# A DeepNorm layer on one core: accumulating transfers of the folded weight chunks begin ahead of a group of seven, and a first down block with one folded chunk more

## The chip, the core and the metric

The kernel runs on one core of one Trainium2 chip. TensorE (PE) multiplies, VectorE (DVE) and ScalarE (ACT) work on tiles in SBUF, GpSimd (POOL) and SyncE (SP) issue transfers. The metric is the device time of one execution in microseconds (us); lower is better. A comparison goes by the median of several runs.

## The reference, cut to what matters

One decoder layer in float32, with 256 tokens, width 2048 and a feed-forward width of 5632:

```python
def swiglu(x, w_gu, w_down):
    g, u = jnp.split(x @ w_gu, 2, axis=-1)
    return (jax.nn.silu(g) * u) @ w_down

h = layer_norm(alpha * h + 0.5 * swiglu(h, w_ffn1_gu, w_ffn1_down), ...)
... # retention and sliding-window attention on h @ w_in, gated and mixed
h = layer_norm(alpha * h + mixed, ...)
h = layer_norm(alpha * h + 0.5 * swiglu(h, w_ffn2_gu, w_ffn2_down), ...)
... # gated input embedding
```

The change touches the two feed-forward networks, `f1` and `f2`.

## The kernel before, in words

**Products.** Every float32 operand is split into a high part (rounded to the matmul's fp32r type) and a low part (what is left). A product is three matmuls into one PSUM sum: low by high, high by high, high by low (`Sum.add`, L431 to L433 in the profile). A weight comes in chunks of 512 KB, 128 x 1024 numbers: SP loads the raw chunk (L119), ScalarE casts the high part and VectorE subtracts it from the raw one (`split`, L105 and L106).

**Units.** The weights are a list, `plan`, of units that are taken in order. Each says how many slots of SBUF its load, its making and its keeping take, and how long TensorE works on it, in products (`time`):
- `Single`: one chunk, time 12.
- `Folded`: one chunk, time 12, whose low part VectorE doesn't make. ScalarE writes the raw chunk times -1 into the low part (L169), and a transfer issued by POOL adds the raw chunk to it, with the type's rounding between (L170). Then ScalarE casts the high part (L171).
- `Seven`: a pair of chunks done by seven products in place of eight, time 21. VectorE makes sums of the raw quarters (L226 to L229), the tiles `u` and `v`; ScalarE casts `h`, `hu`, `hv` and `b`, VectorE subtracts `l`, `lu`, `lv` and `b`.
- `Prepared`: a pair whose sums were put in DRAM earlier.

**Blocks.** The gate-up product runs over 11 blocks `j` of 512 columns of the hidden layer; each has 8 pairs of chunks along the width (one chunk of the pair for gate, one for up). The order of pairs from block 1 of `f1` on is "FFSSFSSP": F is a `Single` and a `Folded`, S a `Seven`, P two `Single`s. A chunk is called `f1_gu_1_1_6`: block 1, up, pair 6. In the profile block numbers are left out of weight names (`lf_gu` is a low part of `f1_gu` or `f2_gu`). The down product has two blocks, with the orders `FIRST_DOWN` and `SECOND_DOWN` over 22 pairs; its chunk `f1_down_1_19` belongs to pair 19. Its sevens are pairs 12 to 19. After the last seven of a block `seven_common` combines the sums (`eve`, `evw`, L550).

**The order.** The program is written in one pass, and each engine does its instructions in the order of writing. `fill`, called after every unit is done with, decides what is written: it makes loaded units while those ready amount to less than 45 products, and loads units while those ready and loaded amount to less than 90, as far as the counted slots go. A real slot of the 46 comes free when its last reader is through; a load waits on SP for that. What is loaded next to what, and what stands ahead of what on ScalarE, VectorE, POOL and SP, so follows from the order of `plan`.

**Other transfers on SP.** After each block the product of gate and up is transposed by a transfer (L189, `mf<-wf`).

Of the kernel before, what the change touches and what calls it, by code (L numbers as in the profile page):

```python
# [9 lines left out]
F32R = mybir.dt.float32r  # L10
# [28 lines left out]
SLOTS = 46  # L39


SEVEN = (0, 1, 2, 3)

AHEAD = {1: (4, 5), 2: (4,), 3: (4, 5), 4: (4,), 5: (4, 5), 6: (4,), 7: (4, 5)}
# [3 lines left out]

SEVEN_DOWN = (6, 7, 8, 9)

FIRST_DOWN = "PPPPPPFFSFSPSFSPSFSSPS"
SECOND_DOWN = "PPPSPSPSFSPSFSSPSPPPPP"
LEAD = 4

# [8 lines left out]
def layer(ctx: ExitStack, tc: tile.TileContext, io):  # L63
# [16 lines left out]
    def slot(shape, dt, name):  # L80
        return slots.tile(shape, dt, tag="slot", name=name)
# [6 lines left out]
    plan = []  # L88

    def chunk_of(key):  # L90


        name, at = key[0], key[1:]
        if name.endswith("_gu"):
            j, gu, c = at
            w = io[name][2 * j : 2 * j + 2, gu, c // 2, :, c % 2 * 2 : c % 2 * 2 + 2, :]
            return w.rearrange("g p k n -> p g (k n)")
        if name[-1] == "2":
            j, c = at
            w = io[name[:-1]][j : j + 2, c // 2, :, c % 2 * 2 : c % 2 * 2 + 2, :]  # L100
            return w.rearrange("g p k n -> p g (k n)")
        return io[name][at]

    def split(dst_hi, dst_lo, src, lo_engine=None):
        act.copy(dst_hi, src)  # L105
        (lo_engine or dve).tensor_tensor(dst_lo, src, dst_hi, ALU.subtract)  # L106

    class Chunk:


        def __init__(self, key, pieces=1, queue=None):
            src = chunk_of(key)
            self.key, self.paired = key, key[0].endswith("_gu") or key[0][-1] == "2"
            self.name = "_".join(map(str, key))
            self.raw = slot(list(src.shape), F32, "r" + self.name)
            n = src.shape[2] // pieces
            self.parts = [slice(j * n, j * n + n) for j in range(pieces)]
            for at in self.parts:
                (queue or sync).dma_start(self.raw[:, :, at], src[:, :, at])  # L119
# [7 lines left out]
        def make(self):  # L127
            self.make_hi()
            split(self.hi, self.lo, self.raw)

        def of(self, v, kk):

            if self.paired:
                return v.rearrange("p g (k n) -> p g k n", k=2)[:, :, kk, :]
            return v[:, kk, :]
# [4 lines left out]
    class Single:  # L140


        loads, makes, keeps, time = 1, 2, 2, 12
# [4 lines left out]
        def load(self, **how):  # L148
            self.chunk = Chunk(self.key, **how)
# [1 line left out]
        def make(self):  # L151
            self.chunk.make()

    class Folded:

        loads, makes, keeps, time = 1, 2, 2, 12

        def __init__(self, key):  # L160
            self.key = key

        def load(self, **how):
            self.chunk = Chunk(self.key, **how)

        def make(self):
            c = self.chunk
            c.make_hi()
            act.mul(c.lo, c.raw, -1.0)  # L169
            pool.dma_start(c.lo, c.raw, accum_op=ALU.add)  # L170
            act.copy(c.hi, c.raw)  # L171

    class Turn:

# [28 lines left out]
    class Seven:  # L203
# [4 lines left out]
        loads, makes, keeps, time = 2, 6, 7, 21  # L208
# [37 lines left out]
    class Prepared:  # L246


        loads, makes, keeps, time = 6, 3, 7, 21
# [63 lines left out]
    loaded, ready = [], []  # L313
    room = {"slots": 0, "used": 0, "ahead": 45, "far": 90, "quiet": False}

    def fill(must=False):

        while True:
            queued = sum(u.time for u in ready)
            left = room["slots"] - room["used"]  # L320
            wanted = must and not ready or not room["quiet"] and queued < room["ahead"]
            if loaded and wanted and loaded[0].makes <= left:
                u = loaded.pop(0)
                u.make()
                room["used"] += u.keeps - u.loads
                ready.append(u)
                continue
            first = loaded[0] if loaded else plan[0] if plan else None
            queued += sum(u.time for u in loaded)
            if plan and queued < room["far"] and plan[0].loads + first.makes <= left:  # L330
                u = plan.pop(0)
                u.load()
                room["used"] += u.loads
                loaded.append(u)
                continue
            return

    def make_next():
        u = loaded.pop(0)
        assert u.makes <= room["slots"] - room["used"]  # L340
        u.make()
        room["used"] += u.keeps - u.loads
        ready.append(u)

    def take(key):
        if not ready:
            fill(True)
        u = ready.pop(0)
        assert u.key == key, (u.key, key)
        return u  # L350
# [23 lines left out]
    def features_chunk(key, n_k, rhs, ps):  # L374
        c, chunks = key[-1], n_k // 4
        u = take(key)
        hi, lo = u.chunk.hi, u.chunk.lo

# [64 lines left out]
    def tokens_out(key, n_k, lhs, ps, n=512, before=None):  # L443

        nk = 1024 // n
        sums = [Sum(ps[t][:, :n], n_k) for t in range(2)]
        for c in range(n_k // nk):
            u = take(key + (c,))
            tokens_chunk(u.chunk, c * nk, lhs, sums, (0, 1), range(nk))
            done(u)  # L450
            run_side()

    def block_units(units, keys):

        for kind, p in units:
            if kind == "P":
                plan.extend(Single(keys(n, p)) for n in range(2))
            elif kind == "F":
                plan.extend(of(keys(n, p)) for n, of in enumerate((Single, Folded)))
            else:  # L460
                plan.append((Seven if kind == "S" else Prepared)(keys(0, p), keys(1, p)))

    def block(name, units, keys, lhs, forms, sums, fold, before=None):
# [5 lines left out]
        for j, (kind, p) in enumerate(units):  # L469
            if before is not None:  # L470
                before(j)
            if kind in "PF":
                for n in range(2):
                    u = take(keys(n, p))
                    tokens_chunk(u.chunk, 2 * p, lhs, [sums[t][n] for t in range(2)], (0, 1))
                    done(u)
                    run_side()
                continue
            u = take(keys(0, p))
            a11, a12 = (half_of(lhs(2 * p + e), 0) for e in range(2))  # L480
            a22 = half_of(lhs(2 * p + 1), 1)
            f5, f6, f7, f3 = forms(p)
            q2, q3, q4 = sums[0][0], sums[0][1], sums[1][0]
            steps = [
                (p1, a11, u.b11), (q2, a12, u.b21), (q3, f3, u.b22), (q5, f5, u.t1),
                (p7, f7, u.t3), (p6, f6, u.t2), (q4, a22, u.t4),
            ]
            if p == sevens[-1]:
                steps = [steps[j] for j in (0, 3, 5, 4, 1, 2, 6)]
            for to, left, right in steps:  # L490
                to.add(left, right)
            done(u)
            run_side()
            if p == sevens[-1]:
                fold(p1.ap, p6.ap, p7.ap, q5.ap)
# [38 lines left out]
    def units_of(order, sevens, ahead=()):  # L534

        sevens, ahead = list(sevens), list(ahead)
        plain = [p for p in range(KD // 2) if p not in sevens + ahead]
        of = {"S": sevens, "D": ahead, "P": plain, "F": plain}
        return [(kind, of[kind].pop(0)) for kind in order]
# [21 lines left out]
    def plan_tokens(key, n_k, nk=2):  # L561
        for c in range(n_k // nk):
            plan.append(Single(key + (c,)))
# [373 lines left out]
    def gu_units(name, j):  # L937
        if j == 0:
            return [("P", p) for p in range(KD // 2)]
        if name == "f2" and j in AHEAD:  # L940
            plain = "P" if j < 4 else "F"
            return units_of(*((f"P{plain}SDSDSP", SEVEN[:3]) if j % 2 else (f"P{plain}SSDSSP", SEVEN)), AHEAD[j])
        order = "FFSSFSSP" if name == "f1" or j > 8 else "PFSSFSSP"
        return units_of(order, SEVEN[: order.count("S")])

# [3 lines left out]
    def down_units(n_held):  # L949
# [4 lines left out]
        first, second = [], []  # L954
        for out, order in ((first, FIRST_DOWN), (second, SECOND_DOWN)):
            n = order.count("S")
# [17 lines left out]
    def ffn(name, i, ht, norm, keep, residual, keepers, away):  # L974
# [33 lines left out]
        for j in range(KF // 4):  # L1008
# [22 lines left out]
            def before(u, j=j, offset=KD // 2 - len(units)):  # L1031
# [7 lines left out]
                if j == 0 and u == 7:  # L1039
                    for g in sorted({p // 2 for p in SEVEN}):  # L1040
                        hi, lo = (slot([P, 8, P], F32R, f"{name}f{w}{g}") for w in "hl")
# [136 lines left out]
    GATE_UNITS = units_of("PPSSPSSP", (0, 1, 2, 3))  # L1178
    RET_UNITS = [units_of(order, SEVEN[: order.count("S")]) for order in ("SPSPSPSP", "PSPSPPPP")]
    gate_keys = lambda b: lambda n, p: ("w_in_f2", 29 + 4 * b + 2 * n, p)  # L1180
# [637 lines left out]
    def warm_up():  # L1818

        ps = bank("warm")  # L1820
        for _ in range(WARM):
            pe.transpose(ps[:, :P], ident, ident)

    with tc.manual_schedule():
# [10 lines left out]
        for blk in range(2, 4):  # L1835
            plan_tokens(("w_pg", blk), KD)
        kept = sorted({p // 2 for p in SEVEN})
        warm_up()
# [105 lines left out]
```

## Time and profile before

| | |
|---|---|
| median of 3 runs | 2230.45 us (2227.97 to 2230.84) |
| the profiled execution | 2230.62 us |
| its span, from the first to the last instruction | 2228.6 us |
| mean granted clock of TensorE | 0.999 |
| TensorE busy | 2218.5 us, 10140 matmuls |
| VectorE busy | 2004.0 us, 90% |
| ScalarE busy | 1439.0 us, 65% |
| GpSimd busy | 50.9 us, 2% |
| moved by DMA | 570.51 MB, mean 256 GB/s |
| accumulating transfers of gate-up chunks | 42 of 512 KB, 8.2 us median from issue to landing |

A stall of TensorE is read where two matmuls that follow each other start further apart than their neighbours. The waits name the instruction that came last before the late one; the chain of waits follows that back to where the delay came from. SPq in a row is SP's queue, where a transfer's issue waits its turn.

### The profile page before, as it was taken

What the parts mean: (1) busy time and instruction counts of PE and PEld (TensorE: products, weight loads), DVE (VectorE), ACT (ScalarE), POOL (GpSimd) and SP (SyncE); (2) the same over time, 40 slices, a digit from 0 to 9 for tenths busy, and PEclk for the clock granted to TensorE, in tenths of its full rate; (3) what the DMA queues carried; (4) which work ended last, traced back from release to release, by engine and by line L of the source; (5) the groups of instructions that cost most, each with busy time, mean ns of one, the idle gap of its engine ahead of it and who ended that gap; (6) DMA issues with size and microseconds to landing.
All of it is one profiled execution on the core that took longest, in us unless ns stands there. A gap on an engine that the chain in (4) does not pass through costs nothing.

```text
span 2228.6 us, 29103 instructions
## 1 busy us (share of the span) xinstructions
PE 2218.5 (100%) x10140; PEld 1838.9 (83%) x10140; DVE 2004.0 (90%) x2624; ACT 1439.0 (65%) x1677; POOL 50.9 (2%) x65
## 2 busy tenths in 40 slices
PE   9999999999999999999999999999999999999998
PEld 8888888888888888888788888888888888888887
DVE  6999999989998789789999888779999999999977
ACT  6777777777565545557865567466766677765653
POOL 0000000000000000000000000000000000000000
PEclk9999999999999999999999999999999999999999
DMA  9988998976686889757976568888999999666871
GB/s 321 250 264 252 249 263 241 269 227 217 228 305 234 298 283 338 203 179 232 291 233 226 184 203 321 316 302 266 301 301 295 300 248 276 209 233 221 309 283 68
DMA packets 302075, 570.51 MB, mean 256 GB/s; under 512 B 98652, under 2 KB 103388, under 8 KB 301928
## 3 DMA queue, kind: packets, MB, share of 16 engines
q1 hardware_dynamic: 291880, 536.71, 72.3%
q0 software_dynamic: 8064, 29.36, 7.0%
q10 hardware_dynamic: 1984, 2.58, 0.4%
q8 instruction: 79, 1.29, 0.2%
q14 instruction: 68, 0.56, 0.1%
HBM read 487.32 MB, written 31.46 MB: 233 GB/s over the span
## 4 chain that ended last, share of the span: by engine, by line
PE 93%; DMA 3%; DVE 2%; issue 1%; ACT 0%; SPq 0%; ACTq 0%; POOL 0%; DVEq 0%; POOLq 0%
PE rqk L382 3%; PE f2g L431 3%; PE f2g L433 3%; PE f2g L432 3%; PE f1g L431 2%; PE f1g L433 2%; PE f1g L432 2%; PE f2u L431 2%; PE f2u L433 2%; PE f2u L432 2%; PE f1u L433 2%; PE f1u L431 2%; PE f1u L432 2%; PE aqk L382 2%; PE f2e L431 1%; PE f1e L431 1%
## 5 line engine op out<-in xcount | busy, mean ns | idle before, releaser
L106 DVE TENSOR_TENSOR lf_gu<-rf_gu,hf_gu 128x1024 fp32r<-128x1024 f32 (+1 forms) x225 | 267.7, 1210 | 22.1 <-ACT hf_gu L105 21.1
L105 ACT CAST hf_gu<-rf_gu 128x1024 fp32r<-128x1024 f32 (+1 forms) x225 | 228.7, 1039 | 22.1 <-DMA rf_gu<-in_f_gu 21.5
L106 DVE TENSOR_TENSOR lw_in_f<-rw_in_f,hw_in_f 128x1024 fp32r<-128x1024 f32 x140 | 167.8, 1219 | 15.0 <-ACT hw_in_f L105 15.0
L106 DVE TENSOR_TENSOR lf_down<-rf_down,hf_down 128x1024 fp32r<-128x1024 f32 x130 | 155.7, 1220 | 12.9 <-ACT hf_down L105 11.1
L105 ACT CAST huf_gu<-uf_gu 128x1024 fp32r<-128x1024 f32 x76 | 80.1, 1053 | 125.4 <-DVE uf_gu L227 109.4
L105 ACT CAST hf_down<-rf_down 128x1024 fp32r<-128x1024 f32 x130 | 132.7, 1049 | 30.5 <-DMA rf_down<-in_f_down 21.3
L105 ACT CAST hw_in_f<-rw_in_f 128x1024 fp32r<-128x1024 f32 x140 | 140.4, 1049 | 2.3 <-PE gt L433 1.6
L105 ACT CAST hvf_gu<-vf_gu 128x1024 fp32r<-128x1024 f32 x76 | 80.1, 1054 | 32.4 <-DVE vf_gu L229 30.5
L106 DVE TENSOR_TENSOR luf_gu<-uf_gu,huf_gu 128x1024 fp32r<-128x1024 f32 x76 | 92.6, 1218 | 0.0
L106 DVE TENSOR_TENSOR lvf_gu<-vf_gu,hvf_gu 128x1024 fp32r<-128x1024 f32 x76 | 92.6, 1218 | 0.0
L431 PE MATMUL f1g<-hf_gu,xt 128*128 128x512 f32 x232 | 90.8, 391 | 0.0
L433 PE MATMUL f1g<-lf_gu,xt 128*128 128x512 f32 x232 | 90.5, 390 | 0.0
L432 PE MATMUL f1g<-hf_gu,xt 128*128 128x512 f32 x232 | 90.5, 390 | 0.0
L431 PE MATMUL f2g<-hf_gu,ht 128*128 128x512 f32 x211 | 82.2, 390 | 0.0
L433 PE MATMUL f2g<-lf_gu,ht 128*128 128x512 f32 x211 | 82.1, 389 | 0.0
L432 PE MATMUL f2g<-hf_gu,ht 128*128 128x512 f32 x211 | 82.1, 389 | 0.0
L433 PE MATMUL f1u<-lf_gu,xt 128*128 128x512 f32 x192 | 75.0, 391 | 1.2 <-DMA lf_gu<-rf_gu 1.2
L431 PE MATMUL f1u<-hf_gu,xt 128*128 128x512 f32 x192 | 74.7, 389 | 0.0
L432 PE MATMUL f1u<-hf_gu,xt 128*128 128x512 f32 x192 | 74.7, 389 | 0.0
L170 POOL DMA_DIRECT2D lf_gu<-rf_gu x42 | 36.4, 867 | 1641.2 <-DMA rf_gu<-in_f_gu 1017.6
L105 ACT CAST huf_down<-uf_down 128x1024 fp32r<-128x1024 f32 x32 | 33.7, 1054 | 60.7 <-DVE uf_down L227 58.7
L1057 ACT ACTIVATE eve<-eve 128x1024 f32<-128x1024 f32 x20 | 21.2, 1061 | 67.3 <-DVE eve L1056 67.3
(1512 smaller groups left out, 6978.3 us busy)
## 6 DMA issues: line engine op xcount, KB each, us to landing
rf_gu<-in_f_gu SPq DMA_DIRECT2D x361, 512.0 KB
rf_down<-in_f_down SPq DMA_DIRECT2D x176, 512.0 KB
rw_in_f<-in_w_in_f SPq DMA_DIRECT2D x148, 512.0 KB
lf_gu<-rf_gu POOLq DMA_DIRECT2D x42, 512.0 KB, 8.2
rw_rv<-in_w_rv SPq DMA_DIRECT2D x32, 512.0 KB
rw_ret<-in_w_ret SPq DMA_DIRECT2D x32, 512.0 KB
rw_mix<-in_w_mix SPq DMA_DIRECT2D x32, 512.0 KB
rw_pg<-in_w_pg SPq DMA_DIRECT2D x32, 512.0 KB
```

The lines of the kernel that those rows point to most:

```text
L105: act.copy(dst_hi, src)
L106: (lo_engine or dve).tensor_tensor(dst_lo, src, dst_hi, ALU.subtract)
L170: pool.dma_start(c.lo, c.raw, accum_op=ALU.add)
L382: pe.matmul(ps[f], hi[:, kk, f * P : (f + 1) * P], rhs(k), start=k == 0, stop=k == n_k - 1,)
L431: pe.matmul(o, al, bh, start=first, stop=False)
L432: pe.matmul(o, ah, bh, start=False, stop=False)
L433: pe.matmul(o, ah, bl, start=False, stop=self.left == 0)
L1057: act.activation(g, g, AF.Silu)
```

## The change

A folded chunk becomes two units. `Folding` loads the raw chunk, has ScalarE write the low part times -1 and POOL issue the accumulating transfer; its time is 0. `Folded` only casts the high part and is taken as before. `fold_at` puts the `Folding` into `plan` ahead of its chunk: 12 products or more ahead, and where there is a `Seven` among the 12 units of `plan` before that place (or at it), ahead of the last such `Seven`. `Folded` stays at the chunk's own place. `fill` passes over units without time. `FIRST_DOWN` gets another order: the first fold comes one pair earlier, there are six F in place of five, and the sevens stand one place earlier or so.

```diff
+FOLD_AHEAD = 12, 12
...
-FIRST_DOWN = "PPPPPPFFSFSPSFSPSFSSPS"
+FIRST_DOWN = "PPPPPFFSFSFSPSFSPSFSPS"
...
-    class Folded:
-        loads, makes, keeps, time = 1, 2, 2, 12
+    class Folding:
+        loads, makes, keeps, time = 1, 1, 2, 0
...
-        def load(self, **how):
-            self.chunk = Chunk(self.key, **how)
+        def load(self):
+            self.chunk = Chunk(self.key)
 
         def make(self):
             c = self.chunk
-            c.make_hi()
+            c.lo = slot(list(c.raw.shape), F32R, "l" + c.name)
             act.mul(c.lo, c.raw, -1.0)
             pool.dma_start(c.lo, c.raw, accum_op=ALU.add)
+
+    class Folded:
+        loads, makes, keeps, time = 0, 1, 2, 12
...
+        def make(self):
+            c = self.chunk = self.begun.chunk
+            c.hi = slot(list(c.raw.shape), F32R, "h" + c.name)
             act.copy(c.hi, c.raw)
+            room["used"] -= self.begun.keeps
+
+    def fold_at(ahead, key):
+        begun = Folding(key)
+        at, time = len(plan), 0
+        while at > 0 and time < ahead:
+            at -= 1
+            time += plan[at].time
+        if ahead and any(isinstance(u, Seven) for u in plan[at - 12 : at + 1]):
+            while not isinstance(plan[at], Seven):
+                at -= 1
+        plan.insert(at, begun)
+        plan.append(Folded(begun))
...
     def make_next():
...
-        ready.append(u)
+        if u.time:
+            ready.append(u)
 
     def take(key):
-        if not ready:
+        while not ready:
             fill(True)
...
             elif kind == "F":
-                plan.extend(of(keys(n, p)) for n, of in enumerate((Single, Folded)))
+                plan.append(Single(keys(0, p)))
+                fold_at(FOLD_AHEAD[keys(1, p)[0][-3:] == "_gu"], keys(1, p))
```

What moves, at three places. First ScalarE in block 1 of `f1`, around the seven of pair 1 and the folded pair 6 behind it. Before:

```order
L105 CAST hf1_gu_1_0_1_576<-rf1_gu_1_0_1_472 128x1024
L105 CAST bf1_gu_1_0_1_580<-rf1_gu_1_1_1_474 128x512
L105 CAST huf1_gu_1_0_1_583<-uf1_gu_1_0_1_570 128x1024
L105 CAST hvf1_gu_1_0_1_587<-vf1_gu_1_0_1_571 128x1024
L105 CAST hf1_gu_1_0_6_607<-rf1_gu_1_0_6_539 128x1024
L169 ACTIVATE lf1_gu_1_1_6_639<-rf1_gu_1_1_6_553 128x1024
L171 CAST hf1_gu_1_1_6_638<-rf1_gu_1_1_6_553 128x1024
```

And with the change:

```order
L170 ACTIVATE lf1_gu_1_1_6_570<-rf1_gu_1_1_6_475 128x1024
L107 CAST hf1_gu_1_0_1_579<-rf1_gu_1_0_1_477 128x1024
L107 CAST bf1_gu_1_0_1_583<-rf1_gu_1_1_1_479 128x512
L107 CAST huf1_gu_1_0_1_586<-uf1_gu_1_0_1_573 128x1024
L107 CAST hvf1_gu_1_0_1_590<-vf1_gu_1_0_1_574 128x1024
L107 CAST hf1_gu_1_0_6_610<-rf1_gu_1_0_6_541 128x1024
L187 CAST hf1_gu_1_1_6_641<-rf1_gu_1_1_6_475 128x1024
```

The negated copy of chunk 1_1_6, with its transfer behind it, has moved from behind the seven's four casts to ahead of them.

Second SP between block 1 and block 2 of `f1`: the loads of the last seven (pair 3), of the last pair (7) and of the next block's folded pairs (4 and 5). Before:

```order
L119 DMA rf1_gu_1_0_3_611<-in_f1_gu 128x2x512
L119 DMA rf1_gu_1_1_3_613<-in_f1_gu 128x2x512
L189 DMA_TRANSPOSE mf10_615<-wf10_555 128x16x128
L119 DMA rf1_gu_1_0_7_643<-in_f1_gu 128x2x512
L119 DMA rf1_gu_1_1_7_687<-in_f1_gu 128x2x512
L119 DMA rf1_gu_2_0_4_722<-in_f1_gu 128x2x512
L119 DMA rf1_gu_2_1_4_743<-in_f1_gu 128x2x512
```

And with the change:

```order
L121 DMA rf1_gu_2_1_4_614<-in_f1_gu 128x2x512
L121 DMA rf1_gu_2_1_5_616<-in_f1_gu 128x2x512
L219 DMA_TRANSPOSE mf10_618<-wf10_555 128x16x128
L121 DMA rf1_gu_1_0_3_643<-in_f1_gu 128x2x512
L121 DMA rf1_gu_1_1_3_645<-in_f1_gu 128x2x512
L121 DMA rf1_gu_1_0_7_647<-in_f1_gu 128x2x512
L121 DMA rf1_gu_1_1_7_691<-in_f1_gu 128x2x512
```

The folded chunks 2_1_4 and 2_1_5 are now loaded ahead of the transposing transfer, and the two chunks of the last seven behind it.

Third SP at the end of the first down block of `f1`. Before:

```order
L119 DMA rf1_down_0_20_4717<-in_f1_down 128x1024
L119 DMA rf1_down_1_20_4777<-in_f1_down 128x1024
L119 DMA rf1_down_0_17_4779<-in_f1_down 128x1024
L119 DMA rf1_down_1_17_4781<-in_f1_down 128x1024
L119 DMA rf1_down_0_18_4803<-in_f1_down 128x1024
L119 DMA rf1_down_1_18_4805<-in_f1_down 128x1024
L119 DMA rf1_down_0_21_4911<-in_f1_down 128x1024
L119 DMA rf1_down_1_21_4938<-in_f1_down 128x1024
L119 DMA rf1_down_0_19_4965<-in_f1_down 128x1024
L119 DMA rf1_down_1_19_4967<-in_f1_down 128x1024
```

And with the change:

```order
L121 DMA rf1_down_1_20_4740<-in_f1_down 128x1024
L121 DMA rf1_down_0_17_4742<-in_f1_down 128x1024
L121 DMA rf1_down_1_17_4744<-in_f1_down 128x1024
L121 DMA rf1_down_0_20_4766<-in_f1_down 128x1024
L121 DMA rf1_down_0_18_4833<-in_f1_down 128x1024
L121 DMA rf1_down_1_18_4835<-in_f1_down 128x1024
L121 DMA rf1_down_0_21_4853<-in_f1_down 128x1024
L121 DMA rf1_down_1_21_4911<-in_f1_down 128x1024
L121 DMA rf1_down_0_19_4913<-in_f1_down 128x1024
L121 DMA rf1_down_1_19_4915<-in_f1_down 128x1024
```

The folded chunk 1_20 is loaded first and 0_20 behind the seven of pair 17, as that seven now stands ahead of pair 20. The last seven's loads (pair 19) keep their place at the end; the slots for them are those of other tiles than before.

More of the change, by code (lines that the diff above doesn't have):

```diff
@@ L152, in make, with __init__, load @@
             self.chunk.make()
-    class Folded:
-        loads, makes, keeps, time = 1, 2, 2, 12
+    class Folding:
+        loads, makes, keeps, time = 1, 1, 2, 0
         def __init__(self, key):
             self.key = key
-        def load(self, **how):
-            self.chunk = Chunk(self.key, **how)
+        def load(self):
+            self.chunk = Chunk(self.key)
         def make(self):
             c = self.chunk
-            c.make_hi()
+            c.lo = slot(list(c.raw.shape), F32R, "l" + c.name)
             act.mul(c.lo, c.raw, -1.0)
             pool.dma_start(c.lo, c.raw, accum_op=ALU.add)
-            act.copy(c.hi, c.raw)
+    class Folded:
+        loads, makes, keeps, time = 0, 1, 2, 12
+        def __init__(self, begun):
+            self.key, self.begun = begun.key, begun
+        def load(self):
+            pass
+        def make(self):
+            c = self.chunk = self.begun.chunk
+            c.hi = slot(list(c.raw.shape), F32R, "h" + c.name)
+            act.copy(c.hi, c.raw)
+            room["used"] -= self.begun.keeps
[10 more added lines that the diff above has]
+        plan.append(Folded(begun))
     class Turn:
@@ L322, in fill @@
             if loaded and wanted and loaded[0].makes <= left:
-                u = loaded.pop(0)
-                u.make()
-                room["used"] += u.keeps - u.loads
-                ready.append(u)
+                make_next()
                 continue
@@ L342, in make_next @@
         room["used"] += u.keeps - u.loads
-        ready.append(u)
+        if u.time:
+            ready.append(u)
     def take(key):
-        if not ready:
+        while not ready:
             fill(True)
```

## The prediction

> **What bounds the kernel now.** I read the page first (busy times), then the waits of TensorE, then the TensorE timeline around each wait, the chain of waits back from there, and last the tables by stretch of time.
>
> Part 1 of the page:
>
> ```profile
> PE 2218.5 (100%) x10140; PEld 1838.9 (83%) x10140; DVE 2004.0 (90%) x2624; ACT 1439.0 (65%) x1677; POOL 50.9 (2%) x65
> ```
>
> PE is busy for 2218.5 of 2228.6 us: 10.1 us of the span are not matmul. Since the change removes no matmul, it can only win time that TensorE loses. The waits of TensorE that the change can reach (released by, us in total, times, longest):
>
> ```profile
> PE f1u L433 <- DMA lf_gu<-rf_gu: 1.2, 2, 0.9
> PE f1e L431 <- DVE evw L550: 0.6, 1, 0.6
> PE f2e L431 <- DVE evw L550: 0.5, 1, 0.5
> ```
>
> The first is a wait for an accumulating transfer (the low part of a folded chunk), the other two are for VectorE at the end of the first down block of either FFN.
>
> Three stretches, each with its length, the busy time (and number) of PE, PEld, DVE, ACT and POOL, then clock, DMA share and GB/s:
>
> ```profile
> 40.00:80.00 40.00, 39.12 (x173) 32.08 (x172) 34.88 (x44) 28.92 (x33) 2.12 (x3) 1.00 1.01 300
> 120.00:160.00 40.00, 40.00 (x178) 33.14 (x177) 37.87 (x46) 29.85 (x34) 2.60 (x3) 1.00 0.91 259
> 540.00:575.00 35.00, 35.00 (x156) 28.81 (x154) 31.29 (x35) 22.09 (x25) 0.86 (x1) 1.00 0.74 243
> ```
>
> The busy time hides part of such a stall, so I measure it from start to start in the TensorE timeline (start us, us, instruction, idle before and its releaser):
>
> ```profile
> 73.21 0.39 PE L431 MATMUL f1u<-hf_gu,xt 128*128 128x512 f32 x1
> 73.43 0.39 PE L432 MATMUL f1u<-hf_gu,xt 128*128 128x512 f32 x1
> 74.70 0.50 PE L433 MATMUL f1u<-lf_gu,xt 128*128 128x512 f32 x1 [0.88 <-DMA lf_gu<-rf_gu]
> 75.04 0.39 PE L431 MATMUL f1u<-hf_gu,xt 128*128 128x512 f32 x1
> ...
> 237.81 0.39 PE L432 MATMUL f1u<-hf_gu,xt 128*128 128x512 f32 x1
> 238.54 0.50 PE L433 MATMUL f1u<-lf_gu,xt 128*128 128x512 f32 x1 [0.34 <-DMA lf_gu<-rf_gu]
> ...
> 401.65 0.39 PE L432 MATMUL f1u<-hf_gu,xt 128*128 128x512 f32 x1
> 401.96 0.50 PE L433 MATMUL f1u<-lf_gu,xt 128*128 128x512 f32 x1
> ...
> 574.81 0.39 PE L433 MATMUL f1e<-lf_down,f1ah 128*128 128x512 f32 x1
> 575.79 0.50 PE L431 MATMUL f1e<-hf_down,f1al 128*128 128x512 f32 x1 [0.59 <-DVE evw L550]
> ...
> 2012.27 0.39 PE L433 MATMUL f2e<-lf_down,f2ah 128*128 128x512 f32 x1
> 2013.18 0.50 PE L431 MATMUL f2e<-hf_down,f2al 128*128 128x512 f32 x1 [0.52 <-DVE evw L550]
> ```
>
> Undisturbed matmuls start 0.22 to 0.23 us apart (73.21 to 73.43; as a mean 40.00 / 178 = 0.225 in the second stretch). The five late ones start 1.27, 0.73, 0.31, 0.98 and 0.91 us after their predecessor, so they are 1.05, 0.50, 0.08, 0.75 and 0.68 us late, together 3.06. The third has no releaser in its row; it is the same matmul of block 9 and I count it with the first two. Each late one lasts 0.50 rather than 0.39 and the next starts 0.34 after it (74.70 to 75.04) rather than 0.225: another 0.11 five times, 0.55. **All five stalls cost 3.6 us, 0.16% of the time.**
>
> **The change part by part.**
>
> *The fold begins earlier.* The chain of waits ahead of the first two stalls (start us, us, what), and the late end of the first down block:
>
> ```profile
> 62.48 0.97 ACT lf_gu L169
> 63.73 10.93 DMA lf_gu<-rf_gu
> ...
> 208.10 9.48 DMA rf_gu<-in_f_gu
> ...
> 229.58 8.92 DMA lf_gu<-rf_gu
> ...
> 557.97 0.03 PE f1d0s L433
> 558.00 5.72 DMA rf_down<-in_f_down
> 563.84 0.69 DVE uf_down L226
> ...
> 573.92 1.22 DVE lf_down L106
> 575.13 0.61 DVE evw L550
> ```
>
> In block 1 the negated copy ran at 62.48 and its transfer took from 63.73 to 74.66; the matmul followed at 74.70. On ScalarE that copy (chunk 1_1_6) stood behind the four casts of the seven before it; now it stands ahead of them. ScalarE runs the four one by one as VectorE makes their sums, so the move is worth the time that a seven takes on TensorE, less what is queued before: 7 products of 3 matmuls of 0.225 us are 4.7 us. The start of the transfer moves from 63.7 to about 59, its end from 74.7 to about 70 at the same length. At 8.92 (block 5) and 10.93 us (block 1), against lateness of 0.50 and 1.05, 4.7 us are ample. So the stalls at 73.43, 237.81 and 401.65 go: 1.63 + 3 × 0.11 = 1.96 us. The landing times of all 42 accumulating transfers of the gate-up blocks:
>
> ```profile
> L169 ACT ACTIVATE lf_gu<-rf_gu x42: 1050/1056/1077, 38.0 to 1870.3; 128x1024 fp32r<-128x1024 f32 x42
> ...
> L170 POOL DMA_DIRECT2D lf_gu<-rf_gu x42: 859/859/1007, 39.4 to 1871.7; - x42
> ...
> DMA to landing us min/median/max: 5.1/8.2/10.9
> ```
>
> At a median of 8.2 and a worst of 10.9, only the third pair of a block ever came too late; the first two pairs had been in time already, so for those the move brings nothing.
>
> *What is moved past.* Each fold issues four things: the load of its raw chunk on SP, the negated copy on ScalarE, the transfer on POOL, and later the cast of the high part. The copy (1.056 us) now stands in ScalarE's queue ahead of the last seven's casts, two of them where both folds of the next block come there, 2.1 us. What hides it (ScalarE and VectorE around the last seven of block 3, and TensorE's use of its last sum):
>
> ```profile
> 153.25 1.05 ACT L105 CAST hf_gu<-rf_gu 128x1024 fp32r<-128x1024 f32 x1
> ...
> 157.51 1.05 ACT L105 CAST huf_gu<-uf_gu 128x1024 fp32r<-128x1024 f32 x1 [2.70 <-DVE uf_gu L227]
> ...
> 156.14 0.68 DVE L226 TENSOR_TENSOR uf_gu<-rf_gu,rf_gu 128x512 f32<-128x512 f32 x1
> ...
> 161.67 1.22 DVE L106 TENSOR_TENSOR lvf_gu<-vf_gu,hvf_gu 128x1024 fp32r<-128x1024 f32 x1
> ...
> 165.28 0.39 PE L433 MATMUL f13s<-lvf_gu,f1fh 128*128 128x512 f32 x1
> ```
>
> ScalarE is idle for 2.70 us before 157.51, in wait for VectorE: two copies at 2.1 us fit in. VectorE's last low part ends at 162.89, 2.39 us ahead of its use at 165.28. So even if the copies pushed all four casts by 2.1 us, nothing would reach TensorE. I put this at nothing; without either cover it would cost at most 2.1 us a block.
>
> On POOL the issue takes 0.86 to 1.01 us, and POOL is 2% busy: nothing. The transfers per FFN grow by one (the first down block folds six chunks, not five). That takes one subtract off VectorE and adds a copy on ScalarE; both lie beside matmuls: nothing.
>
> *On SP* the raws of the next block's folded chunks now go ahead of the last seven's raws, and these come behind the transposing transfer. SP around the place in before:
>
> ```profile
> 132.83 3.84 SPq L119 DMA_DIRECT2D rf_gu<-in_f_gu  x4
> 140.80 2.91 SPq L189 DMA_TRANSPOSE mf<-wf  x1
> 143.81 23.45 SPq L119 DMA_DIRECT2D rf_gu<-in_f_gu  x12
> ```
>
> The last seven's raws were among the four that started at 132.83; now they start behind the transposing at about 143.8, when the following raws start now. At the landing time of 5.72 us that a raw took above they are there at 149.5, at the longest shown, 9.48, at 153.3. ScalarE reads the first at 153.25 and VectorE at 156.14. So the raws arrive in time, but a margin of 11 us has become one of about 4 us.
>
> The DMA engines are full from 40 to 80 us (share 1.01) and nearly so later (0.91). An early fold then doesn't only gain: while it moves its 512 KB, raw loads in the same stretch may land later. I bound this between nothing (the total of bytes is the same but for two transfers) and the 10.93 us of the slowest transfer for a raw, which the margins in the rows above just hold; I take the middle of 5.72 and 9.48, about 7.5 us. A rule speaks here against the change: by the Trainium skill, "DMA: Bandwidth & Descriptors", section "Issuing engines are not separate DMA queues", transfers of all issuing engines run on the same 16 DMA engines and interleave, so that issuing from POOL doesn't keep a fold out of the way of SP's loads. The trace agrees where it shows the share of 1.01 and the 10.93 us in the same 40 us; by this rule alone the gain would be smaller by what the displaced loads cost.
>
> *The first down block.* In the chain above a matmul of the seven of pair 17 ends at 557.97 and frees a slot, the raw of the last seven (pair 19) starts at 558.00, lands at 563.72, and VectorE starts on it at 563.84. VectorE had been idle before that (the row of its timeline):
>
> ```profile
> 563.84 0.69 DVE L226 TENSOR_TENSOR uf_down<-rf_down,rf_down 128x512 f32<-128x512 f32 x1 [3.29 <-DMA rf_down<-in_f_down]
> ```
>
> It had waited 3.29 us for that raw. From there the chain runs through VectorE to `evw`, which ends at 575.74; TensorE starts at 575.79. Now the seven of pair 17 stands ahead of the folded pair 20 on TensorE, and the loads of pair 19 behind fewer others. In matmuls counted between release and use, its two raws gain 18, 4.1 us, against 0.75 late. The DMA engines have room there (share 0.74 in the third stretch). So this stall goes, 0.75 + 0.11, and its twin in the other FFN, 0.68 + 0.11: 1.65 us. What is late next there is `evw` itself, which then waits for TensorE's sums and ScalarE's copy rather than for VectorE's queue. **Sum**: 1.96 + 1.65 = 3.6 us at most; 0.2 off for what remains of a lateness somewhere, 3.4. The profiled execution took 2230.62 us (0.17 above the median of the runs, 2230.45), so **2227.2 us**.
>
> **The rivals.**
>
> *Slower: the last sevens starve.* The mechanism is the displaced raw load: issued behind two folded raws and the transposing transfer, and into DMA engines that an early fold fills. It decides where the landing takes over 153.25 − 143.8 = 9.5 us for ScalarE, or 12.3 us for VectorE plus the 2.39 us left at TensorE: about 14.7 us. Then TensorE waits in the last seven of each gate-up block with folds at its end, some 17 of them. At 0.5 us each this is 8.5 us: 2230.62 − 3.4 + 8.5 = 2235.7. For it: the full DMA share, and the 9.48 us that a raw took before. Against: 14.7 us is beyond every landing shown. Chance 0.15.
>
> *No change: the stall only moves.* The third pairs arrive in time, but VectorE is 34.88 to 37.87 of 40 us busy, and another low part becomes the late one in the same blocks. TensorE then loses again 2 to 3 us: 2229.5 to 2231. For it: VectorE at 37.87 of 40. Against: its queue loses work rather than gains any, and the 2.39 us above. Chance 0.12.
>
> That the change doesn't do what it says I exclude: the order of the instructions shows the copies ahead of the sevens.
>
> **How the numbers follow.** Forecast, stalls gone: 0.68, with a range of its own of 2224.4 (lowest run before, 2227.97, less 3.6) to 2229.5. Slower rival 0.15, no change 0.12, something not seen here 0.05. The three runs of before span 2.87 us; 0.2%, 4.46 us, is about what a measurement of this kernel can tell from no change. Faster by that means below 2225.99, 1.2 us under the forecast: the stalls alone don't reach it, a low run does. Of the forecast's 0.68 I give 0.24 to faster and 0.44 to same; with 0.12 same, 0.15 slower, and the unseen 0.05 split 0.02, 0.01, 0.02: faster 0.26, same 0.57, slower 0.17. The range runs from 2224.4 up into the slower rival, to where 17 blocks lose 0.4 us each (6.8): 2230.62 − 3.4 + 6.8 = 2234.0.
>
> **What would show it.** Right: the waits of TensorE no longer list the transfer of `lf_gu`, nor `evw` at the end of the first down blocks; the copies of the third pairs begin near 58 us rather than 62.48 in block 1; the first load of pair 19 starts near 554. Wrong: new waits of TensorE in the last sevens, with releasers VectorE or ScalarE that had waited for a raw load of over 10 us; a landing time of the accumulating transfers well above the median of 8.2; or the same five stalls at the same length.

## The result, and the profile after

The changed kernel takes 2243.32 us (median of 22 runs, 2228.89 to 2266.1), the kernel before 2228.88 (22 runs, 2226.1 to 2233.15). The ratio is 1.0064, with a 95% interval of 1.005 to 1.0077: slower by 0.6%, where 0.1 to 0.2% faster was forecast. Besides, the runs spread over 37 us in place of 7. The highest, 2266.1, counts as a slow run and isn't in the ratio; the other 21 spread over 31 us. The profiled execution is one of the higher ones: 2253.94 us, with a span of 2252.2.

Busy times (part 1 of the page) and the waits of TensorE, with the change:

```profile
PE 2226.0 (99%) x10140; PEld 1843.7 (82%) x10140; DVE 2000.9 (89%) x2622; ACT 1440.8 (64%) x1679; POOL 52.6 (2%) x67
...
PE f1u L461 <- DMA lf_gu<-rf_gu: 10.5, 2, 7.6
PE f17s L461 <- DVE lf_gu L108: 4.3, 1, 4.3
PE f11s L461 <- DVE lf_gu L108: 2.2, 1, 2.2
```

Both waits for `evw` are gone, as forecast. Of the three for the third accumulating transfer, the two of blocks 5 and 9 are gone; that of block 1 has grown, and block 7 has one of 7.6 us that was none before. Behind each of the two comes a wait in the same block's last seven. TensorE's timeline in block 1 and block 7:

```profile
73.63 0.39 PE L460 MATMUL f1u<-hf_gu,xt 128*128 128x512 f32 x1
76.87 0.50 PE L461 MATMUL f1u<-lf_gu,xt 128*128 128x512 f32 x1 [2.85 <-DMA lf_gu<-rf_gu]
...
85.91 0.39 PE L460 MATMUL f11s<-hf_gu,xt 128*128 128x512 f32 x1
88.52 0.50 PE L461 MATMUL f11s<-lf_gu,xt 128*128 128x512 f32 x1 [2.23 <-DVE lf_gu L108]
...
327.27 0.39 PE L460 MATMUL f1u<-hf_gu,xt 128*128 128x512 f32 x1
335.30 0.79 PE L461 MATMUL f1u<-lf_gu,xt 128*128 128x512 f32 x1 [7.64 <-DMA lf_gu<-rf_gu]
335.89 0.63 PE L459 MATMUL f1u<-hf_gu,xt 128*128 128x512 f32 x1
...
345.17 0.39 PE L460 MATMUL f17s<-hf_gu,xt 128*128 128x512 f32 x1
349.86 0.50 PE L461 MATMUL f17s<-lf_gu,xt 128*128 128x512 f32 x1 [4.29 <-DVE lf_gu L108]
```

What block 7 costs is read from the matmuls done in 40 us, before and after (a stretch, its length, busy time and number for PE, PEld, DVE, ACT, POOL, then clock, DMA share, GB/s):

```profile
320.00:360.00 40.00, 40.00 (x178) 33.10 (x178) 37.73 (x47) 30.60 (x33) 2.62 (x3) 1.00 0.90 255
```

```profile
0.00:320.00 320.00, 312.52 (x1362) 257.06 (x1363) 278.94 (x334) 228.54 (x249) 18.95 (x27) 0.99 0.92 258
320.00:360.00 40.00, 27.29 (x94) 21.05 (x93) 20.55 (x25) 16.35 (x17) 1.77 (x2) 0.79 1.08 201
```

94 matmuls instead of 178: 84 × 0.225 = 18.9 us lost in one block. Up to 320 us 1362 stand against 1394 before, 7.2 us, nearly all of it in block 1 (54 against 84 from 70 to 90 us). Together 26; the span grew by 23.6, and the stalls that went give about the difference back. Part of the loss is the clock: granted 0.79 here on average. After the 7.64 us of idling the matmuls start 0.43 to 0.59 us apart (335.30, 335.89, 336.32) rather than 0.225. By the Trainium skill, "TensorE: Matmul & The Clock Gate", section "Part 1: The HAM clock gate (the "warmup" mystery)", an idle window of about 3.4 us halves TensorE's clock; the trace agrees, with a granted clock of 0.54 and 0.50 from 330 to 340 us in the rows below.

Block 7 by 5 us with the change:

```profile
310.00:315.00 5.00, 5.00 (x23) 4.14 (x23) 4.93 (x7) 5.00 (x6) 0.86 (x1) 1.00 0.74 203
315.00:320.00 5.00, 5.00 (x23) 4.13 (x22) 5.00 (x6) 4.63 (x6) 0.00 (x0) 1.00 1.24 186
320.00:325.00 5.00, 5.00 (x23) 4.13 (x22) 4.86 (x8) 2.63 (x3) 0.00 (x0) 1.00 1.41 45
325.00:330.00 5.00, 2.66 (x12) 1.88 (x10) 2.34 (x3) 1.39 (x2) 1.77 (x2) 1.00 1.18 71
330.00:335.00 5.00, 0.00 (x0) 0.00 (x0) 0.00 (x0) 0.00 (x0) 0.00 (x0) 0.54 1.48 39
335.00:340.00 5.00, 4.70 (x11) 3.73 (x12) 0.00 (x0) 0.00 (x0) 0.00 (x0) 0.50 0.70 158
```

The two last numbers of a row tell it: from 320 to 335 us the times of the packets add up to more than the 16 DMA engines have (1.18 to 1.48), and yet only 39 to 71 GB/s are moved, where 255 were usual in this stretch before. Which transfers had begun by then is in SP's and POOL's rows, first before, then with the change:

```profile
305.82 5.05 SPq L189 DMA_TRANSPOSE mf<-wf  x1
...
311.64 0.86 POOL L170 DMA_DIRECT2D lf_gu<-rf_gu  x1 [17.73 <-ACT lf_gu L169]
```

```profile
313.04 4.87 SPq L219 DMA_TRANSPOSE mf<-wf  x1
318.01 36.81 SPq L121 DMA_DIRECT2D rf_gu<-in_f_gu  x12
...
313.15 0.86 POOL L171 DMA_DIRECT2D lf_gu<-rf_gu  x1 [26.35 <-DVE lvf_gu L108]
...
DMA to landing us min/median/max: 5.4/8.7/22.1
```

Before, the third accumulating transfer of a block began 5.8 us behind the transposing transfer and right behind the end of its issue. Now both start within 0.11 us of each other, and the accumulating one takes 22.1 us, the longest of all (10.9 was the longest before). From 318 to 335 us the transfer queues show (packets by size; then for each queue its packets, MB and share of the 16 engines' time):

```profile
DMA packets 1314, 0.87 MB, mean 51 GB/s; under 512 B 1160, under 2 KB 1160, under 8 KB 1313
...
q1 hardware_dynamic: 1170, 0.34, 96.4%
q0 software_dynamic: 143, 0.52, 35.8%
```

q1 is SP's queue: nearly all its packets are the small ones of the transposing transfer, and of the raw loads behind them hardly a packet moves. Together the queues move 51 GB/s, a fifth of the usual 255. q0 holds the accumulating transfer. The raws of the last seven, issued from 318.01 on, so come some 25 us after their issue (ScalarE's timeline and the chain):

```profile
343.39 1.05 ACT L107 CAST hf_gu<-rf_gu 128x1024 fp32r<-128x1024 f32 x1 [17.00 <-DMA rf_gu<-in_f_gu]
...
319.23 26.49 DMA rf_gu<-in_f_gu
```

My first theory, **A**: where the accumulating and the transposing transfer move data at once, both collapse, and with them the loads queued behind. Its rivals: **B**, the displaced raw loads of the last sevens are the cost in themselves; **C**, the first down block's new order.

### The profile page after: what moved, and what is told of

The parts are those of the page before. It is cut to its first block, busy times and chain, and to the rows that moved or that the text cites. A ratio compares the mean times of both kernels' runs of the same rounds, so it can differ in the third digit from the quotient of the medians.

```text
span 2252.2 us, 29136 instructions
## 1 busy us (share of the span) xinstructions
PE 2226.0 (99%) x10140; PEld 1843.7 (82%) x10140; DVE 2000.9 (89%) x2622; ACT 1440.8 (64%) x1679; POOL 52.6 (2%) x67
## 4 chain that ended last, share of the span: by engine, by line
PE 92%; DVE 3%; DMA 3%; issue 1%; ACT 0%; SPq 0%; ACTq 0%; DVEq 0%
DMA rf_gu<-in_f_gu 3%; PE rqk L410 3%; PE f2g L459 3%; PE f2g L461 3%; PE f2g L460 3%; PE f2u L459 2%; PE f2u L461 2%; PE f2u L460 2%; PE f1g L461 2%; PE f1g L459 2%; PE f1g L460 2%; PE f1u L460 2%; PE f1u L461 2%; PE f1u L459 2%; PE aqk L410 2%; PE f2e L460 1%
## 5 line engine op out<-in xcount | busy, mean ns | idle before, releaser
L108 DVE TENSOR_TENSOR lw_in_f<-rw_in_f,hw_in_f 128x1024 fp32r<-128x1024 f32 x140 | 167.8, 1219 | 14.8 <-ACT hw_in_f L107 14.6
L108 DVE TENSOR_TENSOR lf_down<-rf_down,hf_down 128x1024 fp32r<-128x1024 f32 x128 | 154.0, 1220 | 16.0 <-ACT hf_down L107 14.3
L461 PE MATMUL f1u<-lf_gu,xt 128*128 128x512 f32 x192 | 76.5, 398 | 10.5 <-DMA lf_gu<-rf_gu 10.5
L256 DVE TENSOR_TENSOR uf_gu<-rf_gu,rf_gu 128x512 f32<-128x512 f32 x76 | 52.1, 686 | 36.6 <-DMA rf_gu<-in_f_gu 36.6
```

The source lines that it names most:

```text
L256: dve.tensor_tensor(t1, b11, b12, ALU.add)
L461: pe.matmul(o, ah, bl, start=False, stop=self.left == 0)
```

## The experiments

**Which part of the change.** Only the first down block changed:

```diff
-FOLD_AHEAD = 12, 12
+FOLD_AHEAD = 12, 0
```

> Only the first down block is changed; the accumulating transfers of gate-up chunks begin where they began before. Theory A (the loss is a collision: an accumulating transfer that moves its data at the same time as the transposing transfer slows both, and the raw loads queued behind them): 2226 to 2229 us, no stall of TensorE over 2 us in the gate-up blocks, and the stall at the end of the first down block gone (1.65 us gained). Theory B (the raw loads of the last sevens are displaced on SP): the same, since they stand where they stood. Theory C (the new order of the first down block costs the time): 2240 or more, spread as wide as with the whole change.

Measured 2227.64 us (2225.43 to 2229.28; ratio 0.9995, 0.9987 to 1.0004). Only the gate-up chunks folded ahead:

```diff
-FOLD_AHEAD = 12, 12
+FOLD_AHEAD = 0, 12
-FIRST_DOWN = "PPPPPFFSFSFSPSFSPSFSPS"
+FIRST_DOWN = "PPPPPPFFSFSPSFSPSFSSPS"
```

> Only the gate-up chunks are folded ahead; the first down block is as before. Theories A and B: 2240 to 2248 us with runs spread over 30 us or so, stalls of TensorE of several us in single gate-up blocks. Theory C: 2227 to 2229.

Measured 2243.64 us (2236.52 to 2252.52; 1.0073, 1.0052 to 1.0094): all of the loss. C falls. In its profile, taken in the fastest of the six runs, one accumulating transfer takes 16.4 us.

**Taking one partner away.** The transposing replaced by a plain transfer of the same bytes:

```diff
-            sync.dma_start_transpose(
...
+            sync.dma_start(
...
```

> The changed kernel, with the transposing transfer replaced by a plain transfer of the same 512 KB between the same tiles (so the hidden layer is left untransposed). SP's order and all bytes are the same. Theory A: the long stalls go, 2225 to 2228 us, runs within 6 us of each other, accumulating transfers land within 11 us. Theory B: no change against the whole change, 2240 to 2246, since the raw loads stand where the change put them.

Measured 2225.53 us (2224.96 to 2226.13; 0.9986, 0.9977 to 0.9994). The loads stand on SP where the change put them, so B doesn't explain the loss. The edit reaches all 38 transposing transfers of the program, 22 of them in the feed-forward networks, so the 3.2 us under before needn't all come from there; but no wait of TensorE for an accumulating transfer is left. The spread shrinks to 1.2 us. It is likely, but not shown, that part of the scatter of the kernel before comes from the transposing transfers too: no run takes them out of it. Its accumulating transfers:

```profile
DMA to landing us min/median/max: 4.8/8.3/10.9
```

The accumulating transfer made plain:

```diff
-            pool.dma_start(c.lo, c.raw, accum_op=ALU.add)
+            pool.dma_start(c.lo, c.raw.bitcast(F32R))
```

> The changed kernel, with the accumulating transfers turned into plain ones of the same bytes on the same queue (so the low part of a folded chunk is the raw chunk). Theory A in the narrow form (it is the adding that collides with the transposing): 2225 to 2228 us and no stall over 2 us. Theory A in the wide form (any transfer issued by POOL beside the transposing one): 2238 to 2246. Theory B: 2240 to 2246.

Measured 2226.92 us (2224.66 to 2229.11; 0.9993, 0.9984 to 1.0001). By the time the narrow form of A holds, but not quite by the landings:

```profile
DMA to landing us min/median/max: 2.9/6.3/14.3
```

A plain transfer from POOL can be caught beside the transposing one too (14.3 against a median of 6.3); it is shorter, and caught less badly, and only 0.5 us of wait is left.

**Making the collision in the kernel before.** There only the transposing transfer is moved, one unit of a block later and then two (`later(DELAY, turn.move)`), and with it ScalarE's two copies of its result (`later(DELAY + 3, joined)`):

```diff
-DELAY = 1
+DELAY = 2
```

> The kernel before, with the transposing transfer written one unit of a block later (DELAY 2 for 1), about 4.7 us; nothing is folded earlier. It then starts about 1 us ahead of the third accumulating transfer of a block, as in the changed kernel, where it started 4 to 7 us ahead. Theory A (collision): slower than before, 2235 to 2245 us, with runs spread over 15 us or more, and accumulating transfers of over 15 us. Theory B (displaced raw loads): within 2 us of 2228.7, since the raw loads keep their places but for one that now goes ahead of the transposing.

> The kernel before, with the transposing transfer two units later (DELAY 3). It is now written behind the third negated copy, and both transfers start within 3 us of each other in most blocks; no load of a fold is moved ahead. Theory A (collision): slower than with DELAY 2 (2235.6), 2240 to 2265 us, several accumulating transfers over 14 us. Theory B: within 3 us of 2228.5.

Measured 2235.63 us with DELAY 2 (2230.76 to 2240.55; 1.0028, 1.0019 to 1.0036) and 2253.76 with DELAY 3 (2250.7 to 2256.95; 1.011, 1.0094 to 1.0125). No load of a fold is moved ahead here, so the collision is enough by itself. DELAY 2 brought the two less close than I had expected: the third accumulating transfers start 2.7 to 7.2 us behind the transposing ones, not 1. One block collapses (14.6 us to landing, a wait of 5.8 us), and the runs spread over 9.8 us, not 15. With DELAY 3, in block 10 (SP, POOL, TensorE, waits):

```profile
429.66 6.59 SPq L189 DMA_TRANSPOSE mf<-wf  x1
...
431.91 0.86 POOL L170 DMA_DIRECT2D lf_gu<-rf_gu  x1 [17.62 <-ACT lf_gu L169]
...
453.93 0.80 PE L433 MATMUL f1u<-lf_gu,xt 128*128 128x512 f32 x1 [13.23 <-DMA lf_gu<-rf_gu]
...
PE f1u L433 <- DMA lf_gu<-rf_gu: 13.2, 1, 13.2
PE f2u L433 <- DMA lf_gu<-rf_gu: 9.9, 1, 9.9
```

Two blocks collapse, though the two transfers start within 2.3 us of each other in 13: not every overlap is a collapse.

**Parting them in the changed kernel.** Three ways: the transposing two units later (`DELAY = 3`), the third fold a seven earlier (`FOLD_AHEAD = 12, 36`), the transposing one unit earlier (`DELAY = 0`).

> The changed kernel, with the transposing transfer two units later (DELAY 3), about 9 us, when the third accumulating transfer has landed (7 to 9 us after its issue where nothing collides); the next block's first two then start 3.5 us behind it. Theory A: 2225 to 2229 us, long stalls gone, if 3.5 us behind is far enough; else still some blocks at 15 us and 2232 to 2240. Theory B: the raws of the last sevens stay displaced behind the two folded raws: 2240 or more.

> The changed kernel, with folds of gate-up chunks 36 products ahead in place of 12: only the third of a block moves, ahead of one seven more, so that its accumulating transfer starts about 4.7 us earlier, 3.5 us ahead of the transposing one. Theory A: fewer overlaps, 2226 to 2235. Theory B: no better than the change, 2240 to 2246, since the loads are where they are with it.

> The changed kernel, with the transposing transfer written one unit earlier (DELAY 0). It waits for ScalarE's copy as it did, so it starts at most 1 us earlier, but the two folded raws now queue behind it on SP and not ahead of it, so that its data no longer wait for 1 MB of raws (some 2.6 us at the 400 GB/s seen). Theory A: its packets are through before the accumulating transfer's begin (about 3 us after that one's issue): 2225 to 2230 us. Theory B: the raws of the last sevens are no earlier: 2240 or more.

Measured 2238.17 us (2229.7 to 2245.75; 1.0042, 1.0027 to 1.0056), 2227.09 (2225.13 to 2229.91; 0.9993, 0.9984 to 1.0001) and 2227.4 (2226.39 to 2228.69; 0.9996, 0.9987 to 1.0004). The last two leave the loads of the last sevens behind the folded raws as the change has them, and the loss is gone: B is refuted once more as its cause. With DELAY 3 `f1` is free of stalls, but in `f2`, where a block's only fold comes at another place, the transposing now meets that one (the two start 0.67 us apart, with 20.4 us to landing at the worst). What TensorE then waits for is ScalarE, which idles 14.28 us for a raw chunk:

```profile
PE f2g L459 <- ACT eve L578: 11.0, 2, 8.9
```

With DELAY 0 (block 7, SP and POOL):

```profile
302.44 1.76 SPq L219 DMA_TRANSPOSE mf<-wf  x1
304.30 8.51 SPq L121 DMA_DIRECT2D rf_gu<-in_f_gu  x7
...
303.73 0.86 POOL L171 DMA_DIRECT2D lf_gu<-rf_gu  x1 [23.80 <-DVE lvf_gu L108]
```

The accumulating transfer still begins 1.3 us behind the start of the transposing one. But that takes 1.76 us on SP instead of 4.87, with the two folded raws behind it and not ahead, and nothing collapses. So starts close together aren't enough; a transposing transfer that is held up on SP seems to belong to it.

The profiles of all versions with both kinds of transfer bear this out. Each accumulating transfer of a gate-up chunk is set against the transposing one nearest to it, by the two starts, the time of the transposing one on SP, and the landing:

| accumulating transfer starts | transposing one on SP | cases | to landing |
|---|---|---|---|
| 0.1 to 3.1 us behind it | 5.0 to 9.3 us | 9 | 11.3 to 22.0 us |
| the same | 4.7 to 4.9 us | 5 | three 7.5 to 8.7 us, two 16.4 and 22.1 |
| the same | up to 4.5 us | 28 | at most 8.9 us |
| 3.4 to 7.3 us behind it | 1.8 to 8.9 us | 79 | at most 10.9 us |
| 0.7 to 3.3 us ahead of it | 5.1 to 8.3 us | 18 | at most 9.2 us |

So the order counts as well: the accumulating transfer is caught where it starts shortly behind a held-up transposing one, and not where it starts shortly ahead.

**The loads alone.** Only the load of a fold goes ahead; the negated copy and the transfer are made where they were before:

```diff
     class Folding:
-        loads, makes, keeps, time = 1, 1, 2, 0
+        loads, makes, keeps, time = 1, 0, 1, 0
...
     class Folded:
-        loads, makes, keeps, time = 0, 1, 2, 12
+        loads, makes, keeps, time = 0, 2, 2, 12
...
+            c.make_hi()
+            act.mul(c.lo, c.raw, -1.0)
+            pool.dma_start(c.lo, c.raw, accum_op=ALU.add)
             act.copy(c.hi, c.raw)
```

> The changed kernel, but of a fold only the load of the raw chunk goes ahead; the negated copy and the accumulating transfer stand again right ahead of the cast of the high part. The raws of the last sevens are displaced on SP as with the whole change, the accumulating transfers start 4 to 7 us behind the transposing one as before it. Theory A (collision): 2227 to 2230 us, with the small waits for the third fold back. Theory B (displaced raw loads): 2240 to 2246.

Measured 2260.71 us (2259.9 to 2263.19; 1.0141, 1.0126 to 1.0157), far from the 2227 to 2230 that I expected of A. The waits:

```profile
PE f2u L460 <- DMA lf_gu<-rf_gu: 9.8, 2, 7.7
PE f1u L460 <- DMA lf_gu<-rf_gu: 5.1, 4, 2.0
PE f1d L460 <- DMA lf_down<-rf_down: 5.0, 1, 5.0
PE f2d L460 <- DMA lf_down<-rf_down: 4.6, 1, 4.6
```

9.6 of these 24.5 us lie in the first down blocks, whose new order needs the earlier fold. The 7.7 us in `f2` are a collapse: the accumulating transfer there started 3.1 us behind a transposing one that took 6.55 us on SP, and landed after 16.5. So A's own premise, that nothing meets, didn't hold. The same for gate-up alone, with the old first down block:

> As the run with only the loads ahead, but for gate-up chunks alone, with the first down block as before the change: it tells what of that run's 32 us is the gate-up blocks'. If the displaced loads themselves cost there (they move while the third accumulating transfer moves, which then lands 8 to 10 us after its issue, 1 to 2 us late in several blocks): 2236 to 2248 us. If that run's loss came from the first down block, whose folds began late in the new order: 2228 to 2232.

Measured 2244.99 us (2240.34 to 2245.98; 1.0067, 1.0055 to 1.008):

```profile
PE f2u L460 <- DMA lf_gu<-rf_gu: 5.7, 1, 5.7
PE f1u L460 <- DMA lf_gu<-rf_gu: 5.3, 4, 1.8
...
DMA to landing us min/median/max: 5.7/8.0/14.5
```

The four waits in `f1` are no collapse: the third folds of blocks 5, 6 and 8 land after 10.3 to 10.5 us and come 1.6 to 1.8 us late, where before block 5 cost 0.3 and the other two nothing; block 1's wait shrank from 0.9 to 0.3. That the displaced raws, which now move beside them, slow them is the likely reason, but only argued. The 5.7 us in `f2` go with the 14.5 us to landing, the same meeting with a transposing transfer as in the run before. So B holds in part: the displaced loads seem to cost a few us, but where the fold begins a seven earlier and nothing collides (2227.09 and 2227.4 above), nothing of it is left.

**Both remedies together**, 36 products ahead and DELAY 0:

> The two remedies together: third fold of a block 36 products ahead and the transposing transfer one unit earlier, ahead of the folded raws. Theory A: no overlap left, 2226 to 2228 us, no stall over 0.4 us in the feed-forward networks; about 0.1% under the kernel before. Theory B: 2240 or more.

Measured 2228.73 us (2228.28 to 2230.44; 1.0002, 0.9993 to 1.001). No collapse, but no sum of gains either, and 0.7 us above the range that I expected: a wait of 1.3 us for a fold of the first down block is new. No version that keeps both kinds of transfer is faster than the kernel before beyond its interval: 2227.09 and 2227.4, the lowest with the whole change, have a ratio of 1 within theirs. Only without transposing is the time clearly lower, by 0.14% (2225.53), and that kernel leaves the hidden layer as it was.

## Why the prediction was wrong, point by point

- **The bound on gains** (3.6 us): it held. The versions without a collapse lie 1.1 to 3.2 us under before, the one with both remedies level with it.
- **The first down block** (1.65 us, by pair 19's loads): the waits for `evw` are gone, and the change of this block alone gives 1.1 us, with a ratio of 1 within its interval. The mechanism was right: in that run the two loads start at 552.36 (forecast: near 554) rather than 558.00, and VectorE begins on them at 557.81 rather than 563.84. The 18 matmuls of lead that the prediction counts stand in none of its rows.
- **The start of the negated copy** (near 58 us in block 1): right. Its transfer began at 58.99 by POOL's row, and it ended at 76.8 by TensorE's, not at 70.
- **The step that failed** is "at the same length". I moved the transfer by 4.7 us and kept its 8.9 to 10.9 us, taking the longest row of before as the bound. With the change it took 17.8 us in block 1 and 22.1 in block 7. The third transfers of a block had been measured where they started 3.6 to 7 us behind the transposing one. Its row, at 140.80, was among those I quoted; that the third fold stood that little behind it, and that a move by about 5 us puts one onto the other, I didn't look for. I counted what each load is moved past on SP's queue, and for POOL only its issue time. That an early fold may slow raw loads I did say, with 10.93 us as the bound; that it meets the transposing transfer I didn't ask, and behind that one a raw took 26.49 us.
- **The rule of the Trainium skill** ("DMA: Bandwidth & Descriptors", "Issuing engines are not separate DMA queues") spoke in the right direction, and the trace goes beyond it: the two didn't only share the engines, together they moved a fifth of the usual rate (51 of 255 GB/s). The section "Rules for kernel authors" of the same page says of a transpose next to ordinary DMAs that it needs nothing. That stands beside a warning of corrupted data; for the time, it doesn't hold here, and not for a plain transfer from POOL either (14.3 us).
- **The slower rival** had place and sign right: the last sevens starve of raws. Its mechanism was another (loads behind a collapsed transposing transfer, 25 us, not loads moved back, at most 9.5), and its form too: in the profiled execution two blocks at 7 and 19 us, not 17 at 0.5. That it would be small I took partly from a margin misread: "a margin of 11 us has become one of about 4 us" goes by a landing of 9.48 us before and of 5.72 after; by 9.48 both times, nothing is left of it on ScalarE (153.3 against 153.25).

Open: how the two hold each other up inside the engines; no run here shows it. The table above tells when it happens, but not why: the collapse may itself lengthen the time on SP, and between 4.7 and 4.9 us both outcomes occur. In the profiled execution of the changed kernel the accumulating transfer starts within 1.3 us behind the transposing one in eight blocks, and two of them collapse.

## What to carry to other kernels

When a transfer is moved in time, its duration is not moved along: list what else is under way at its new place, from all queues, and above all transfers of another kind (here one in packets of under 512 B). The lengths in a profile hold for the neighbours they were measured with. A spread of the runs that grows more than fourfold can be the sign of a collision, as here (though the two versions with the largest losses, 2260.71 and 2253.76, spread over 3 and 6 us only, in four runs each): look for the block where the DMA share is over 1 and the GB/s collapse.

## What was not expected of the hardware

A transposing transfer of 512 KB, with an accumulating one of 512 KB begun 0.1 to 3.1 us behind it, can hold the DMA engines for some 15 us at 39 to 71 GB/s, and the accumulating one then landed after up to 22.1 us, against a median of 8.2 before. Begun shortly ahead of it, it landed within 9.2 us. A plain transfer from POOL is caught too, but less: 14.3 us at the worst. And with every transposing transfer made plain the runs of the changed kernel lie within 1.2 us of each other.
